# Sixteen blocks and eight products at a time, GpSimd work in pieces, and the first four destination blocks counted during the first pass

## The chip, the cores and the metric

The kernel runs on one core of a Trainium2 chip. The metric is the device time of one execution in microseconds. The kernel before has a median of 342.41 us over 4 runs (341.04 to 345.19). Lines such as L539 are lines of the kernel before, unless the text says otherwise. PE is TensorE (PEld its weight loads), DVE is VectorE, ACT is ScalarE, POOL is GpSimd, SP is SyncE.

## The reference

There are 4096 nodes with 128 features each in fp32, and 65536 edges with random ends. Each edge adds the features of its source node to the output row of its destination node:

```python
for i in range(len(edge_index_src)):
    output[edge_index_dst[i]] += node_features[edge_index_src[i]]
```

## The kernel before, in words

The kernel does no gather. It sorts the edges into cells of a 32 by 32 grid (128 source nodes by 128 destination nodes per cell), builds for each cell a count matrix by a matmul of one-hots, and multiplies the transposed features by these counts. Two passes do the sorting; both count with matmuls and move with matmuls by one-hot permutations.

**First pass, by destination block.** The 512 edge columns are handled in six quads (q = 0 to 5) of four groups of up to 22 columns. For a quad, `oh1s` compares the destination block with 32 numbers (L201, tile oh1) and sums columns on PE into `pst`; `scan` runs along them on DVE; `counts` makes running counts in PSUM (`psc`, L234 and L238), which ACT evicts (L241) and which PE sums to ranks (`psr`, L246); `spread1` multiplies the one-hots by the two payloads (L262). `move1` then does, for l = 0 to 3, three compares of ranks on DVE (L283, tile p), calls `meanwhile(l)`, and permutes with 21 or 22 matmuls into `psm` (L286). ACT copies `psm` to `sa` (a code of the source and destination within a block) and `sbk` (the source block, plus one), L290 and L291. `sbk` of all six quads is what the second pass starts from.

**Second pass, by source block.** The 32 destination blocks are taken in groups of 4, 4, 4, 4, 8 and 8 (`GROUPS`). For a group of four, `buckets4` compares `sbk` with 32 numbers (L473), `payloads` multiplies by `sa` (L415; on DVE for group 0, on POOL otherwise), `column_sums`, `sums_to_each` and `counts_ranks` give ranks (L482, L489, L496, L499, L502, `ranks` L432), `permutations` compares ranks with numbers (tiles p2a and p2c) and `permuted` moves the payloads by matmuls (L452). `quad_keys` splits the result into the low seven bits of both ends (L465, slo and dlo). The groups of eight count with 32 compares (L400), matmuls (L408), a running sum on DVE (L423) and a mask on POOL (L427).

**Block loop.** There are 32 slots: four for each four destination blocks, each with eight source blocks (32 cells). `onehots(slot)` makes two compares of 4096 columns on DVE (L201, tile oh). `blocks` multiplies them for one source block and the four destination blocks (four matmuls) into a PSUM bank `psa` (L532), and ACT casts the bank to the tile a (L534). `product` multiplies features (a high and a low part) by a into `pso` (L539), always for the slot before. A slot issues two `blocks`, four product matmuls, and so on, four times. After four slots, `evacuate` copies `pso`, and `finish` transposes it (psx, L305), copies it and sends it out by a DMA on SP.

**What sets the order.** All is scheduled by hand: each engine runs its instructions in the order in which the program text issues them, with semaphores between engines. The second pass's steps are spread over the slots by the table `STEPS` (L28): a step's first function is issued ahead of the slot's blocks, its second one behind the products, the third two slots later. Ahead of the loop, group 0 and the start of group 1 are written out (L565 to L581). Tiles with the same tag share a buffer. PSUM has two buffers each of the tags psA, pso and misc, and one each of psi and ps2. The permutation compares and the block one-hots read their numbers from PSUM (psi).

Of the kernel before, what the change touches and what calls it, by code (L numbers as in the profile page):

```python
# [8 lines left out]
P = 128  # L9
# [69 lines left out]
def _fast(ctx, tc, X, src32, dst32, out, ident, fmax, flag_i, T):  # L79
# [129 lines left out]
    def oh1s(q):  # L209

        if q % 2 == 0:
            oh1[q // 2] = sb1.tile([P, 2, NL, NB], BF16, name="oh1", tag=f"o{q // 2}")
        onehot(oh1q(q), kd[:, q], NL, NB)
        pst = ps.tile([P, 512], F32, name="pst", tag="pso")
        for j in range(NJ):
            PE.matmul(out=pst[:, j:j + 1],  # L216
                      lhsT=oh1q(q)[:, 4 * j:4 * j + 4, :].rearrange("p l b -> p (l b)"),
                      rhs=ones[:, :1], start=True, stop=True)
        sums[q] = pst
# [8 lines left out]
    def counts(q):  # L228

        cum = sb1.tile([P, NB, NL], BF16, name="cum", tag=f"c{q % 2}")  # L230
        for j0 in range(0, NJ, 4):
            n = min(4, NJ - j0)
            psc = ps.tile([P, 512], F32, name="psc", tag="psA")
            PE.matmul(out=psc[:, :n * P], lhsT=early[:],  # L234
                      rhs=oh1q(q)[:, 4 * j0:4 * (j0 + n), :].rearrange("p t b -> p (t b)"),
                      start=True, stop=j0 + n == 1)
            for j in range(max(j0, 1), j0 + n):
                PE.matmul(out=psc[:, (j - j0) * P:(j - j0 + 1) * P],  # L238
                          lhsT=sums[q][:, j - 1:j].to_broadcast([P, P]), rhs=identb[:],
                          start=False, stop=j == j0 + n - 1)  # L240
            S.activation(out=cum[:, :, 4 * j0:4 * (j0 + n)], func=RELU, bias=minus[:],  # L241
                         in_=psc[:, :n * P].rearrange("p (t b) -> p b t", b=NB))
            yield
        psr = ps.tile([P, 512], F32, name="psr", tag="pso")
        for b in range(NB):
            PE.matmul(out=psr[:, :NL], lhsT=identb[:], rhs=cum[:, b, :],  # L246
                      start=b == 0, stop=b == NB - 1)
        rank1[q] = sb2.tile([P, 4, NJ, 2], BF16, name="rank1", bufs=3)
        for k in range(2):
            S.copy(out=rank1[q][:, :, :, k], in_=psr[:, :NL].rearrange("p (j l) -> p l j", l=4))  # L250
# [25 lines left out]
    def move1(q, meanwhile):  # L276
        psm = ps.tile([P, 512], F32, name="psm", tag="misc")
        for l in range(4):
            t = p1[l // 2]
            n = len([j for j in range(NJ) if j * NCH + q * 4 + l < T])  # L280
            for j0, j1, m0, m1 in WIN:
                j1 = min(j1, n)
                onehot(t[:, l % 2, j0:j1, m0:m1], rank1[q][:, l, j0:j1], j1 - j0, m1 - m0, m0=m0)  # L283
            meanwhile(l)
            for j in range(n):
                PE.matmul(out=psm[:, l * 64:(l + 1) * 64], lhsT=t[:, l % 2, j, :],  # L286
                          rhs=v1[q][:, 4 * j + l].rearrange("p k b -> p (k b)"),
                          start=j == 0, stop=j == n - 1)
        pv = psm[:, :256].rearrange("p (l k b) -> p l k b", l=4, k=2)
        S.copy(out=sa[:, place(q), :], in_=pv[:, :, 0, :])  # L290
        S.copy(out=sbk[:, place(q), :], in_=pv[:, :, 1, :])  # L291
# [9 lines left out]
    def finish():  # L301
        for k, res in done:
            psx = ps.tile([P, 512], F32, name="psx", tag="misc")
            for i in range(4):
# [33 lines left out]
    clear(p2a)  # L338

    def during(q):  # L340

        def step(l):
            if l == 0:
                if q + 2 < NQ and q == 0:
# [8 lines left out]

    for q in range(NQ):
        move1(q, during(q))
        if q + 2 < NQ:
# [7 lines left out]

    p2c = sb1.tile([P, 2, NCH, P], BF16, name="p2c", tag="o2")
    clear(p2c)
    p2b = [p2a[:, 0], p2a[:, 1], p2c[:, 0], p2c[:, 1]]
    first = [sum(GROUPS[:g]) for g in range(len(GROUPS))]
    keys2 = {}

    def pass2(g):
# [12 lines left out]
        def tiles():  # L384
            if g == 0:
                both = sb1.tile([P, 2] + shape[1:], BF16, name="vc2", tag="o0")
                T2["v"], T2["c"] = both[:, 0], both[:, 1]
                T2["o"] = sb1.tile(shape, BF16, name="oh2", tag="o1")[:]
            else:
                at = -(g - 1) % 3  # L390
                tags = ("c0", "o1", "o0")
                T2["o"] = sb1.tile(shape, BF16, name="oh2", tag=tags[at])[:]
                T2["c"] = sb1.tile(shape, BF16, name="cum2", tag=tags[(at + 1) % 3])[:]
                T2["v"] = sb1.tile(shape, BF16, name="v2", tag="F" if g % 2 == 0 else "c1")[:]

# [8 lines left out]
        def before_all():  # L404
            psb = ps.tile([P, 512], F32, name="psb", tag="misc")
            for h in range(2):
# [3 lines left out]
            for h in range(2):  # L410
                S.copy(out=flat2(T2["c"])[:, h * NH], in_=psb[:, h * W:(h + 1) * W])

        def payloads():
            for i in range(gk):
                (V if g == 0 else G).tensor_tensor(out=T2["v"][:, :, i], in0=T2["o"][:, :, i], op=OP.mult,  # L415
                                in1=sa[:, :, None, d0 + kk * i:d0 + kk * i + kk].to_broadcast(
                                    [P, NCH, NB, kk]))

# [7 lines left out]
        def masked():  # L426
            G.tensor_tensor(out=flat2(T2["c"]), in0=flat2(T2["c"]), in1=flat2(T2["o"]), op=OP.mult)  # L427

        def ranks():
            psr = ps.tile([P, 512], F32, name="psr2", tag="misc")  # L430
            for s in range(NB):
# [13 lines left out]

        def permuted(i):
            if i % 4 == 0:
                T2["ps2"] = ps.tile([P, 512], F32, name="ps2", tag="ps2", bufs=1)
# [11 lines left out]
        def quad_keys(i):  # L460
            ks = [sb2.tile([P, 4 * NB, 2], U16, name=n) for n in ("slo2", "dlo2")]
            pau = T2["pa"][:].bitcast(U16).rearrange("p s d -> p (s d)")[
                :, :, None].to_broadcast([P, 4 * NB, 2])
            for t, arg, op in zip(ks, (7, 127), (OP.logical_shift_right, OP.bitwise_and)):
                V.tensor_single_scalar(out=t[:], in_=pau, scalar=arg, op=op)  # L465
            keys2[(d0 + i) // 4] = ks
            if i == 0:
                V.tensor_reduce(out=fmax[:, g:g + 1], in_=T2["r"][:, :, :, 0], op=OP.max,
                                axis=AX.XY)

# [8 lines left out]
        def column_sums():  # L479
            T2["p"] = ps.tile([P, 512], F32, name="pst2", tag="misc")  # L480
            for c in range(NCH):
# [10 lines left out]
        def counts_ranks():  # L492
            for c0 in range(0, NCH, 4):
                psc = ps.tile([P, 512], F32, name="psc2", tag="psA")
                cs = [c for c in range(c0, c0 + 4) if c % NH]
# [25 lines left out]
    def onehots(slot):  # L521

        oh = sb1.tile([P, 2, 4 * 8, P], BF16, name="oh", tag=f"t2{slot % 2}")
        at = slot % 4 * 32
        for k, io in ((0, piotas), (1, piota)):
            onehot(oh[:, k], keys2[slot // 4][k][:, at:at + 32], 32, io=io)
        return oh

    def blocks(k, oh, a):
        psa = ps.tile([P, 512], F32, name="psa", tag="psA")  # L530
        for i in range(4):
# [10 lines left out]
    def flag():  # L542
# [9 lines left out]
        V.tensor_reduce(out=fall[:], in_=fmax[:, :ng + 1], op=OP.add, axis=AX.X)  # L552
        psf = ps.tile([P, 512], F32, name="psf", tag="misc")
        PE.matmul(out=psf[:1, :1], lhsT=fall[:], rhs=one[:], start=True, stop=True)
        V.tensor_single_scalar(out=flag_i[:], in_=psf[:1, :1], scalar=float(P * T),
                               op=OP.not_equal)

    todo = [pass2(g) for g in range(len(GROUPS))]

# [4 lines left out]

    (vec, mat), (vec1, mat1), pair0, pair1 = todo[0]  # L565
    vec()
    mat()
    nvec, nmat = todo[1].pop(0)
    nvec1, nmat1 = todo[1].pop(0)
    vec1()  # L570
    mat1()
    nvec()
    nmat()
    pair0[0]()
    pair0[1]()
    nvec1()
    pair1[0]()
    pair1[1]()
    pair1[2]()
    oh = onehots(0)  # L580
    nmat1()  # L581
    slots = NB
    prev, pso = None, None
    late = {}
    for slot in range(slots):
# [5 lines left out]
        if slot + 1 < slots:  # L591
            oh = onehots(slot + 1)
        run(st[0] for st in steps)
        a = sb1.tile([P, 8, 4 * P], F32R, name="a", tag=f"A{slot % 2}")
        if slot % 4 == 0:
            pso = ps.tile([P, 512], F32, name="pso", tag="pso")
        for k in range(0, 8, 2):
            blocks(k, cur, a)
            blocks(k + 1, cur, a)
            if prev is not None:  # L600
                product(k, *prev)
                product(k + 1, *prev)
            if k == 0:
                finish()
        if prev is not None and prev[0] % 4 == 3:
# [100 lines left out]
```

## Time and profile before

| | |
|---|---|
| Median of 4 runs | 342.41 us (341.04 to 345.19) |
| The profiled execution | 340.93 us, its span 339.2 us |
| Busy share of the span | PE 89%, DVE 83%, ACT 59%, POOL 25% |
| Chain that ended last | PE 68%, DVE 19%, ACT 5%, issue 4%, DMA 1% |
| Mean granted clock of PE | 0.968 |
| The last `sbk` copy starts | 71.20 us |
| One-hots of slot 0 start | 87.99 us |
| Blocks of slot 0, 1, 3 start | 93.53, 101.06, 120.24 us |
| Last product group starts | 328.45 us |

The chain that ended last is followed back from the last instruction, at each step to what released it. Busy shares are means over stretches with different limits, so the timeline and the busy times of single stretches say more than the shares. A DVE or ACT row's mean is the time of one instruction; PE's matmuls overlap, so the distance between their starts says what one costs in a run.

### The profile page before, as it was taken

The page shows a single profiled execution, that of the slowest core. Times are in us where ns is not written, and L with a number is a line of the kernel's source. Part 1 is how long each engine was busy: PE and PEld are TensorE (multiplying, and loading weights), DVE is VectorE, ACT ScalarE, POOL GpSimd, SP SyncE. Part 2 cuts the span into 40 slices and gives each one's busy share as a digit, 9 for nine tenths or more (in the row PEclk, how much of TensorE's full clock was granted, in tenths as well). Part 3 has the DMA queues.
Part 4 walks back from the last instruction along what each step waited for, and adds up shares of the span by engine and source line. Part 5 has one row for each costly group of instructions (what it writes and reads, how often), then busy time and mean ns, then how long its engine had stood idle before and what let it go on. Part 6 is the DMA issues. An engine that isn't in the chain of part 4 may idle for free.

```text
span 339.2 us, 8630 instructions
## 1 busy us (share of the span) xinstructions
PE 302.3 (89%) x3784; PEld 239.2 (71%) x3784; DVE 280.4 (83%) x365; ACT 201.6 (59%) x389; POOL 84.0 (25%) x47
## 2 busy tenths in 40 slices
PE   0689899668879899999999999999999999999993
PEld 0468777456667588677788787778877778777772
DVE  4999999983899839849999898999999779868700
ACT  2776545014556856755765776575576676677761
POOL 6627000206014060000898000069900000000000
PEclk9999979858799999999999999999999999999999
DMA  8500000000000000100010000001000100100101
GB/s 240 131 2 5 2 3 2 2 2 0 5 2 0 2 2 2 31 2 3 0 33 2 0 31 5 2 1 33 2 1 4 30 2 0 33 2 0 33 2 33
DMA packets 8711, 5.81 MB, mean 17 GB/s; under 512 B 224, under 2 KB 8416, under 8 KB 8672
## 3 DMA queue, kind: packets, MB, share of 16 engines
q1 hardware_dynamic: 8528, 4.72, 4.9%
q8 instruction: 30, 0.49, 0.6%
q10 hardware_dynamic: 144, 0.52, 0.6%
q14 instruction: 9, 0.07, 0.1%
HBM read 3.15 MB, written 2.10 MB: 15 GB/s over the span
## 4 chain that ended last, share of the span: by engine, by line
PE 68%; DVE 19%; ACT 5%; issue 4%; DMA 1%; DVEq 0%; ACTq 0%
PE pso L539 33%; PE psa L532 15%; DVE oh L201 8%; PE ps L452 7%; PE psr L432 3%; PE psm L286 3%; DVE p L201 2%; DVE v L262 2%; ACT cum L502 2%; DMA raw<-in_edge_index_dst_dram 1%; DVE cum L423 1%; ACT cum L241 1%; PE psr L246 1%; PE psc L496 1%; DVE oh L400 1%
## 5 line engine op out<-in xcount | busy, mean ns | idle before, releaser
L534 ACT CAST a<-psa 128x512 fp32r<-128x512 f32 x256 | 137.7, 591 | 46.3 <-PE psa L532 45.3
L539 PE MATMUL pso<-a,xr 128*128 128x512 f32 x512 | 149.3, 414 | 0.0
L201 DVE TENSOR_TENSOR oh<-psi,slo 128x4096 bf16<-128x4096 uint16 x32 | 73.1, 2285 | 27.9 <-PE psa L532 27.9
L539 PEld LDWEIGHTS pso<-a,xr 128*128 128x128 f32 x512 | 87.0, 189 | 11.4
L532 PE MATMUL psa<-oh 128*128 128x128 bf16 x1024 | 81.2, 220 | 1.4 <-ACT a L534 0.9
L532 PEld LDWEIGHTS <-oh 128*128 128x128 bf16 x1024 | 59.3, 98 | 30.0 <-issue 28.4
L201 DVE TENSOR_TENSOR oh<-psi,dlo 128x4096 bf16<-128x4096 uint16 x32 | 72.9, 2279 | 0.0
L415 POOL TENSOR_TENSOR v<-oh,sa 128x3072 bf16<-128x3072 bf16 x7 | 37.7, 5397 | 40.3 <-DVE oh L473 31.9
L427 POOL TENSOR_TENSOR cum<-cum,oh 128x6144 bf16<-128x6144 bf16 x2 | 23.9, 11938 | 75.8 <-ACT a L534 75.8
L201 DVE TENSOR_TENSOR p<-psi,rank 128x448 bf16<-128x448 uint16 (+3 forms) x72 | 29.2, 472 | 0.0
L241 ACT ACTIVATE cum<-psc,minus 128x512 bf16<-128x512 f32 (+1 forms) x36 | 21.8, 649 | 10.6 <-PE psc L238 10.3
L286 PE MATMUL psm<-v,p 128*128 128x64 bf16 x512 | 23.0, 204 | 5.3 <-DVE p L201 4.8
L286 PEld LDWEIGHTS <-p 128*128 128x128 bf16 x512 | 20.1, 105 | 7.1 <-DVE p L201 6.9
L201 DVE TENSOR_TENSOR p2a<-psi,rank 128x768 bf16<-128x768 uint16 x32 | 15.5, 546 | 5.6 <-ACT rank L437 5.6
L238 PEld LDWEIGHTS <-sums 128*128 128x128 bf16 x126 | 11.3, 107 | 6.3 <-issue 3.2
L201 DVE TENSOR_TENSOR p2c<-psi,rank 128x768 bf16<-128x768 uint16 x32 | 15.5, 544 | 0.0
L234 PE MATMUL psc<-oh,early 128*128 128x512 bf16 (+1 forms) x36 | 14.6, 406 | 0.9 <-ACT cum L241 0.9
L190 POOL TENSOR_TENSOR xr<-xf,xr 128x512 fp32r<-128x512 f32 x8 | 11.8, 1494 | 13.3 <-ACT xr L186 13.3
L452 PEld LDWEIGHTS <-p2a 128*128 128x128 bf16 x384 | 12.8, 100 | 3.0 <-DVE p2a L201 1.8
L216 PE MATMUL pst<-ones,oh 128*128 128x1 bf16 x132 | 4.3, 164 | 11.6 <-DVE oh L201 11.5
L238 PE MATMUL psc<-identb,sums 128*128 128x128 bf16 x126 | 14.4, 240 | 0.0
L452 PEld LDWEIGHTS <-p2c 128*128 128x128 bf16 x384 | 12.9, 102 | 1.8 <-issue 1.5
(82 smaller groups left out, 273.2 us busy)
## 6 DMA issues: line engine op xcount, KB each, us to landing
xf<-in_node_features_dram SPq DMA_DIRECT2D x4, 512.0 KB, 7.4
out_dram<-rows SPq DMA_DIRECT2D x8, 256.0 KB, 2.3
raw<-in_edge_index_src_dram ACTq DMA_DIRECT2D x1, 512.0 KB, 4.8
raw<-in_edge_index_dst_dram SPq DMA_DIRECT2D x1, 512.0 KB, 5.0
```

The costliest lines, as they stand in the source:

```text
L190: G.tensor_tensor(out=xr[i // 2][:, bs, 1, :], op=OP.subtract, in0=xf[i][:, h * BX // 2:(h + 1) * BX // 2], in1=xr[i // 2][:, bs, 0, :])
L201: V.tensor_tensor(out=dst.rearrange("p i (m k) -> p i m k", k=2), in0=io.rearrange("p i (m k) -> p i m k", k=2), in1=keys2[:, :, None, :]. ...
L234: PE.matmul(out=psc[:, :n * P], lhsT=early[:], rhs=oh1q(q)[:, 4 * j0:4 * (j0 + n), :].rearrange("p t b -> p (t b)"), start=True, stop=j0 + ...
L238: PE.matmul(out=psc[:, (j - j0) * P:(j - j0 + 1) * P], lhsT=sums[q][:, j - 1:j].to_broadcast([P, P]), rhs=identb[:], start=False, stop=j = ...
L241: S.activation(out=cum[:, :, 4 * j0:4 * (j0 + n)], func=RELU, bias=minus[:], in_=psc[:, :n * P].rearrange("p (t b) -> p b t", b=NB))
L286: PE.matmul(out=psm[:, l * 64:(l + 1) * 64], lhsT=t[:, l % 2, j, :], rhs=v1[q][:, 4 * j + l].rearrange("p k b -> p (k b)"), start=j == 0, ...
L415: (V if g == 0 else G).tensor_tensor(out=T2["v"][:, :, i], in0=T2["o"][:, :, i], op=OP.mult, in1=sa[:, :, None, d0 + kk * i:d0 + kk * i + ...
L427: G.tensor_tensor(out=flat2(T2["c"]), in0=flat2(T2["c"]), in1=flat2(T2["o"]), op=OP.mult)
L452: PE.matmul(out=ps2[:, d % 4 * NB:(d % 4 + 1) * NB], lhsT=p2b[d % 4][:, c, :], rhs=T2["v"][:, c, d // kk, :, d % kk], start=c == 0, stop=c ...
L532: PE.matmul(out=psa[:, i * P:(i + 1) * P], lhsT=oh[:, 0, 4 * k + i, :], rhs=oh[:, 1, 4 * k + i, :], start=True, stop=True)
L534: S.copy(out=a[:, k, :], in_=psa[:])
L539: PE.matmul(out=pso[:], lhsT=xr[s // 16][:, s % 16, v, :], rhs=a[:, k, :], start=s == 0 and v == 0, stop=s == NB - 1 and v == 1)
```

## The change

Four things change.

1. **Sixteens and eights.** A slot issues four `blocks` (sixteen matmuls), then the products of four k (eight matmuls), twice. `psA` gets four buffers, and `pso`, `misc` and the first pass's other PSUM tags get one. `pst` of the first pass alternates between the tags ps2 and pso, `psr` uses psA. `finish` comes behind the second sixteen blocks.
2. **GpSimd in pieces.** The multiplies of groups 1 to 5 are put into a list as pieces of four columns, the masks of the groups of eight as pieces of two; `little` issues up to seven per slot, and what is left before it is needed.
3. **Group 0 quad by quad.** Group 0 no longer goes through `pass2`. While `move1` works on quads 2 to 5, `beside(q, l)` issues the bucket compares, the multiplies (on POOL, the last quad's on DVE), column sums, scans and counts of the quads that are done, and in quad 5 the ranks and the permutations of the first two destination blocks for five of the six quads. The last quad's part follows the first pass, and its result is added to the earlier part (`part0`).
4. **Head of the loop.** `onehots(0)` is made in four halves of 16, ahead of group 1's scan on DVE; group 1's `counts_ranks` come behind it. `p2c` is cleared before quad 5's move.

```diff
-        pst = ps.tile([P, 512], F32, name="pst", tag="pso")
+        pst = ps.tile([P, 512], F32, name="pst", tag=("ps2", "pso")[q % 2], bufs=1)
...
-            psc = ps.tile([P, 512], F32, name="psc", tag="psA")
+            psc = ps.tile([P, 512], F32, name="psc", tag="psA", bufs=4)
...
-        psm = ps.tile([P, 512], F32, name="psm", tag="misc")
+        psm = ps.tile([P, 512], F32, name="psm", tag="misc", bufs=1)
...
+    def buckets0(q):
+        cs = place(q)
+        V.tensor_tensor(
+            out=T0["o"][:, cs], op=OP.is_equal,
...
+        (G if q < NQ - 1 else V).tensor_tensor(
+            out=T0["v"][:, cs], in0=T0["o"][:, cs], op=OP.mult,
+            in1=sa[:, cs, None, :4].to_broadcast([P, 4, NB, 4]))
+        for c in range(cs.start, cs.stop):
+            PE.matmul(out=T0["p"][:, c:c + 1], rhs=ones[:, :1], start=True, stop=True,
+                      lhsT=T0["o"][:, c].rearrange("p s k -> p (s k)"))
...
+    def ranks0(cs):
+        n = cs.stop - cs.start
+        psr = T0["p"][:, 64 + 4 * cs.start:64 + 4 * cs.stop]
+        for s in range(NB):
+            PE.matmul(out=psr, lhsT=identb[:], rhs=T0["c"][:, cs, s, :],
+                      start=s == 0, stop=s == NB - 1)
+        for k in range(2):
+            S.copy(out=T0["r"][:, :, cs, k], in_=psr.rearrange("p (c d) -> p d c", d=4))
...
+    def beside(q, l):
+
+        if q == 2 and l == 2:
+            start0()
+            buckets0(0)
+            buckets0(1)
+        if q == 2 and l == 3:
+            scan0(0)
+            scan0(1)
+        if q == 3 and l == 0:
+            counts0(0)
+            counts0(1)
+        if q in (3, 4):
+            if l == 1:
+                buckets0(q - 1)
+            if l == 2:
+                scan0(q - 1)
+            if l == 3:
+                counts0(q - 1)
+        if q == 5:
+            if l == 0:
+                buckets0(4)
+                for cs in EARLY0:
+                    ranks0(cs)
+            if l == 1:
+                scan0(4)
+                counts0(4)
+                for cs in EARLY0:
+                    permute0((0, 1), cs)
+            if l == 2:
+                ranks0(place(4))
+            if l == 3:
+                permute0((0, 1), place(4))
+                permuted0((0, 1), done0, 0)
...
         def payloads():
             for i in range(gk):
...
+                for c in range(0, NCH, 4):
+                    small.append(((g, 1), lambda i=i, c=c: payload(i, slice(c, c + 4))))
...
         def masked():
-            G.tensor_tensor(out=flat2(T2["c"]), in0=flat2(T2["c"]), in1=flat2(T2["o"]), op=OP.mult)
+            for c in range(0, NCH, 2):
+                small.append(((g, 0), lambda c=c: G.tensor_tensor(
+                    out=flat2(T2["c"])[:, c:c + 2], in0=flat2(T2["c"])[:, c:c + 2],
+                    in1=flat2(T2["o"])[:, c:c + 2], op=OP.mult)))
...
-    (vec, mat), (vec1, mat1), pair0, pair1 = todo[0]
-    vec()
-    mat()
+    last0 = place(NQ - 1)
+    buckets0(NQ - 1)
+    scan0(NQ - 1)
+    counts0(NQ - 1)
+    for cs in done0:
+        permute0((2, 3), cs)
     nvec, nmat = todo[1].pop(0)
     nvec1, nmat1 = todo[1].pop(0)
-    vec1()
-    mat1()
     nvec()
+    ranks0(last0)
+    permuted0((2, 3), done0, 0)
+    parts = [T0["x"][:, i * P:(i + 1) * P].rearrange("p (d s) -> p s d", d=4) for i in range(2)]
+    part0 = sb1.tile([P, NB, 4], BF16, name="part0")
+    S.copy(out=part0[:], in_=parts[0])
+    for d in range(4):
+        permute0((d,), last0)
+        permuted0((d,), (last0,), P)
+    pa0 = sb2.tile([P, NB, 4], BF16, name="pa")
+    V.tensor_tensor(out=pa0[:], in0=parts[1], in1=part0[:], op=OP.add)
     nmat()
-    pair0[0]()
-    pair0[1]()
+    put_keys(0, pa0)
+    oh = onehots(0)
     nvec1()
-    pair1[0]()
-    pair1[1]()
-    pair1[2]()
-    oh = onehots(0)
     nmat1()
+    most_rank(0, T0["r"])
...
         run(st[0] for st in steps)
+        little(7)
...
-        for k in range(0, 8, 2):
-            blocks(k, cur, a)
-            blocks(k + 1, cur, a)
+        for k0 in (0, 4):
+            for k in range(k0, k0 + 4):
+                blocks(k, cur, a)
+            if k0 == 4:
+                finish()
             if prev is not None:
-                product(k, *prev)
-                product(k + 1, *prev)
-            if k == 0:
-                finish()
+                for k in range(k0, k0 + 4):
+                    product(k, *prev)
```

## The prediction

> **What bounds the kernel now.** I read the page's rows, then the stretches of the span, then the chain that ended last, then the timeline of the places that the change touches. The rows of the block loop:
>
> ```profile
> L534 ACT CAST a<-psa 128x512 fp32r<-128x512 f32 x256 | 137.7, 591 | 46.3 <-PE psa L532 45.3
> L539 PE MATMUL pso<-a,xr 128*128 128x512 f32 x512 | 149.3, 414 | 0.0
> ...
> L532 PE MATMUL psa<-oh 128*128 128x128 bf16 x1024 | 81.2, 220 | 1.4 <-ACT a L534 0.9
> ```
>
> PE's two matmul groups hardly wait (0.0 and 1.4 us), while ACT waits 45.3 us for them. The stretches (columns: stretch, us, busy us of PE, PEld, DVE, ACT, POOL, then PE's granted clock):
>
> ```profile
> 0.00:65.60 65.60, 45.93 (x914) 38.02 (x914) 60.15 (x99) 33.78 (x67) 19.82 (x34) 0.97 0.19 50
> 65.60:94.00 28.40, 22.41 (x356) 17.93 (x357) 20.66 (x34) 9.43 (x20) 8.15 (x5) 0.71 0.01 2
> ...
> 246.00:328.00 82.00, 81.95 (x823) 63.30 (x821) 63.93 (x51) 59.03 (x112) 0.10 (x1) 1.00 0.04 11
> ```
>
> So there are three regimes: a first pass bound by DVE (60.15 of 65.60), a transition bound by latency with PE at clock 0.71, and a block loop where PE is full. Inside the loop, one period of the timeline:
>
> ```profile
> 280.07 0.62 PE L532 MATMUL psa<-oh 128*128 128x128 bf16 x8
> ...
> 280.50 1.18 PE L539 MATMUL pso<-a,xr 128*128 128x512 f32 x4
> ...
> 281.52 0.62 PE L532 MATMUL psa<-oh 128*128 128x128 bf16 x8
> ...
> 328.24 4.41 PEld L539 LDWEIGHTS pso<-a,xr 128*128 128x128 f32 x20
> ```
>
> Eight blocks and four products take 281.52 - 280.07 = 1.45 us. The last 20 products, unbroken, take 4.63 us in the chain: 0.2315 each. Blocks in a run start 0.056 us apart. 8 x 0.056 + 4 x 0.2315 = 1.374, so each change from blocks to products and back costs about 0.072 us. From the chain in the transition:
>
> ```profile
> 79.10 1.27 ACT vc L502 x2
> 80.42 1.55 PE psr L432 x32
> 83.14 1.93 PE ps L452 x48
> 85.15 1.95 PE ps L452 x48
> 87.99 6.22 DVE oh L201 x3
> ```
>
> The first one-hots of the second pass start at 87.99. Group 1's counts run under them (86.92 to 93.7), slot 0's blocks start at 93.53, slot 1's at 101.06.
>
> **What the Trainium skill says.** TensorE: Matmul & The Clock Gate, "What's actually happening": the array runs at half clock unless it was busy in a free-running window of 3413 ns. The trace agrees: asked window by window, the clock is 0.50 from 65.05 to 78.70 and from 85.5 to 88.9 (multiples of 3.41), after windows with idle PE. SBUF — State Buffer, "Who interferes with whom": DVE tensor_scalar in a 2-port mode and GpSimd exclude each other for a whole instruction. The trace agrees:
>
> ```profile
> L415 POOL TENSOR_TENSOR v<-oh,sa 128x3072 bf16<-128x3072 bf16 x7 | 37.7, 5397 | 40.3 <-DVE oh L473 31.9
> ```
>
> ```profile
> L465 DVE TENSOR_SCALAR dlo<-pa x8: 281/285/5461, 87.6 to 296.1; 128x256 uint16<-128x256 uint16 x8
> ```
>
> Twice (179.8 and 240.8) dlo took 5.46 us, the length of one POOL multiply. PSUM — Partial Sum Buffer, "Specifications (TRN2)": 8 banks. Before: psi 1, psA 2, pso 2, misc 2, ps2 1; after: psi 1, psA 4, the others 1, so doubled buffers elsewhere are the price of psA's four.
>
> **The change, part by part** (sum against the profiled execution: span 339.2 us, 340.93 us in all, median of the runs 342.41).
>
> Sixteens and eights. Slots 1 to 31 lose two of their four changes each: 31 x 2 x 0.072 = -4.5 us.
>
> Four psA banks. Slots without extra work last 5.79 us; slots 7, 11, 15, 19 and 30 last 6.04, 5.91, 6.03, 5.98 and 6.00, as rank and psb copies sit ahead of the evictions with two banks only. With four I take -0.8 of the 1.0. The counts of a group stay bound by ACT (six evictions in 4.01 us, back to back), so they gain 0. DVE gets 0.9 us more lead per slot (the last block now precedes eight products, not four), so the short DVE waits of slots 14 and 16 (0.24, 0.26) give -0.2.
>
> Single pso, misc and ps2. pso is next written after 16 blocks, 0.90 us, or after a permutation's 1.5 us more; its eviction takes 0.585 plus some 0.25 of latency: 0, at worst 0.1 x 7. finish moves from the first blocks of a slot to behind its second sixteen, so seven of the eight output DMAs are issued on SP some 3 us later, beside the loop (2.3 us to landing); the last stays where it was: 0. psx in slot 5 needs misc free of the column sums: DVE's scan comes some 1.4 us into the slot, psx at 3.7: 0.
>
> GpSimd in pieces. The two dlo stalls fall from 5.46 to about 0.9 us each (5.397 / 6). Worth 0: DVE sat idle 1.21 us before 191.02 and 0.48 before 251.13 for PE, and PE's slots 11, 12, 19 and 20 show no wait. Piece overhead is not in the trace; even 0.2 x 24 us per large group hides before slot 10's ranks (the 11.9 us mask ends at 174.4, its ranks start at 183.4).
>
> Group 0 in the first pass. Rates: a compare of 512 columns 0.33 us on DVE (3072 in 1.67, 768 in 0.465), of 256 0.20; a scan 0.1; a 32-column matmul 0.031; rank copies 0.4 a pair; an eviction 0.69.
> - Quads 2 to 4, DVE: 2 x 0.33 + 2 x 0.1, then twice 0.33 + 0.1: +1.7; quad 5's first permutation compare starts at 67.35, not 65.62. PE has slack there; its column sums wait for DVE, not DVE for them. POOL's new multiplies (0.9 each) are done before the next spread of payloads on DVE, which otherwise would lose up to 0.9 (the spreads at 27.89 and 30.06, beside POOL, took 2.25 and 2.69, not 1.61).
> - Quad 5: bucket 0.33, scan 0.1. PE: column sums at 68.85, then 64 rank matmuls (2.05) and ACT: ranks at 70.75 and 71.75, for which DVE waits about 1.0. Four compares (1.3) and the remaining nine of the pass: done 74.75. Quad 4's counts, eviction, 32 rank matmuls and copies end at about 75 (warm), two compares at 75.2. In PE's order permuted0's 40 matmuls (1.25) stand ahead of the pass's last 21, which wait for them: psm ends near 77.3 against 71.0, sbk is ready at 77.8 against 71.47: +6.3. At half clock the 64- and 512-column matmuls double: up to +1.7. I take +0.8.
> - Tail from sbk: compare 0.4, sums 0.25, scan 0.2, counts 0.45, eviction 0.7, 32 rank matmuls 1.2, copies 0.4; meanwhile DVE does 1.7 of compares and group 1's buckets (1.67). Last permutations, their matmuls and the add: put_keys 5.8 us after sbk. POOL's first pieces run then, so slo waits about half a piece and dlo a whole one: +1.4, with the two themselves 0.5. One-hots start 7.7 us after sbk: near 86.3, against 87.99: 1.7 earlier.
> - But group 1's scan now stands behind one-hot 0 on DVE (4.5 us in four halves), and group 1's counts and ranks stand ahead of slot 0's blocks on PE. Before, they ran under the one-hots. So the counts start at about 91.0, ranks come 7.2 later (86.92 to 94.14 before): 98.2. The halves thus hide nothing. Then DVE: permutations 1.86, group 2's buckets 1.67, and PE's sums 0.7: slot 1 at about 102.7, against 101.06. Slot 0's blocks, 3.9 us with two banks, are under it.
> Sum of this part: +1.7 us, and both ends: -1 (all warm, POOL out of the way) to +7 (cold, with DVE waits on each round trip).
>
> Total: -4.5 - 0.8 - 0.2 + 1.7 = -3.8 us: span 335.4; from the median, 338.6.
>
> **The rivals.**
> - B, the transition costs nothing or gains up to 2 us: the clock rises early since PE has dense small matmuls from 68.9, and slo and dlo meet no piece. For: 2.05 us of unbroken rank matmuls fall into one window. Against: clock 0.50 from 65.05 to 78.70 before, even with a busy PE. Time 334 to 337.
> - C, it costs 3.5 to 7: cold clock in quad 5 (+1.7, 0.9 over mine) and again under group 1's counts (six of 0.86 against 0.67 each: +1.2; ranks +1.0), and DVE waits of 1 us more. Time 340 to 345.8. For: PE stands idle some 5 us ahead of those counts.
> - D, slower: the place is quads 2 to 5, where about twelve new round trips DVE to PE to DVE lie in two strict queues. If each makes DVE wait 0.8 us (compare to sum to scan took that order at 73.3 to 74.97), DVE loses 9 to 10 us, and the time is 346 to 349. It decides once those waits exceed 6.9 us beyond the 1.0 counted, as -5.5 + 1.7 + 6.9 = +3.1. Against: in quads 2 to 4 a triple of compares (1.19) separates each sum from its scan, and the column sums take 0.1 to 0.3.
> - That fewer changes do not help: if the 0.072 belonged to the run of products itself, 8 would cost as much per product as 4. The run of 20 at 0.2315 speaks against; it would add 4.5: 343. It is inside C's range.
>
> **How the numbers follow.** The forecast, 337 to 340: 0.42. B 0.26, C 0.25 (with the last rival), D 0.07. Over 1% faster means below 339.0, which is about what a measurement of this kernel tells from no change: B and a little more than half of the forecast, 0.50. Within 1%: the rest of it and C, 0.43. Slower 0.07. The range leaves out D, the top of C and the bottom of B: 334.5 to 343.5; the likeliest case alone is 337 to 340.
>
> **What would show it.** Plain slots (22, 23, 26 to 28) at 5.64 us, not 5.79; slots 11, 15, 19 equal to them; sbk's last copy near 78.6; one-hot 0 near 86.3; ranks of group 1 near 98.2; slot 1 near 102.7; dlo never above 1.9 us. I am wrong if a plain slot stays at 5.79, or if slot 1 starts before 100 or after 106.

## The result and the profile after

The changed kernel takes 341.99 us (median of 42 runs, 340.54 to 343.35), the kernel before 342.39 (63 runs on the same chips): ratio 0.9976, 95% interval [0.9961, 0.9991]. So the change is worth 0.8 us by the ratio (0.3 to 1.3 us by its interval), where 3.8 were forecast. The profiled execution of the changed kernel took 342.55 us, its span is 341.0; the profiled one of before happened to be the shorter (340.93). I therefore take totals from medians and ratios, and the traces only for where the time lies. Line numbers are now those of the changed kernel, for an experiment those of its own text.

The costliest rows of the page of the changed kernel, to be held against those of before:

```profile
L659 ACT CAST a<-psa 128x512 fp32r<-128x512 f32 x256 | 131.6, 603 | 47.2 <-PE psa L657 47.1
L664 PE MATMUL pso<-a,xr 128*128 128x512 f32 x512 | 133.6, 403 | 0.0
...
L657 PE MATMUL psa<-oh 128*128 128x128 bf16 x1024 | 70.5, 223 | 0.2
...
L535 POOL TENSOR_TENSOR v<-oh,sa 128x512 bf16<-128x512 bf16 x42 | 42.6, 1052 | 37.2 <-DVE oh L596 26.1
L552 POOL TENSOR_TENSOR cum<-cum,oh 128x512 bf16<-128x512 bf16 x24 | 29.5, 1250 | 68.1 <-DVE cum L547 34.7
...
L581 PE MATMUL ps<-v,p2a 128*128 128x32 bf16 x336 | 12.2, 195 | 6.2 <-DVE p2a L201 6.2
...
L547 DVE TENSOR_TENSOR cum<-cum,oh 128x512 bf16<-128x512 bf16 x22 | 16.1, 731 | 1.5 <-ACT cum L531 0.8
```

Products and blocks wait no longer than before (0.0 and 0.2 us). The loss sits in two small rows: the permutation matmuls of the second pass (L581) waited 6.2 us for their one-hots p2a on DVE, and an addition of the running sum (L547) takes 731 ns in the mean. The same two rows of the kernel before:

```profile
L452 PE MATMUL ps<-v,p2a 128*128 128x32 bf16 x336 | 12.1, 194 | 0.3 <-DVE p2a L201 0.3
...
L423 DVE TENSOR_TENSOR cum<-cum,oh 128x512 bf16<-128x512 bf16 x22 | 9.3, 425 | 0.7
```

The timeline of the changed kernel shows how the two hang together (columns: start, us, engine, line, operation, tiles, count; in brackets the idle time before and its releaser):

```profile
157.79 8.40 DVE L547 TENSOR_TENSOR cum<-cum,oh 128x512 bf16<-128x512 bf16 x11 [0.84 <-ACT cum L531]
158.81 1.33 POOL L552 TENSOR_TENSOR cum<-cum,oh 128x512 bf16<-128x512 bf16 x1 [31.77 <-DVE cum L547]
...
165.80 9.21 POOL L552 TENSOR_TENSOR cum<-cum,oh 128x512 bf16<-128x512 bf16 x8 [0.36 <-DVE cum L547]
166.10 2.28 DVE L201 TENSOR_TENSOR oh<-psi,slo 128x4096 bf16<-128x4096 uint16 x1
...
170.50 1.94 DVE L201 TENSOR_TENSOR p2a<-psi,rank 128x768 bf16<-128x768 uint16 x4
171.10 1.94 PE L581 MATMUL ps<-v,p2a 128*128 128x32 bf16 x48 [2.92 <-DVE p2a L201]
```

Before, the mask was one GpSimd instruction and followed the sum:

```profile
157.27 5.02 DVE L423 TENSOR_TENSOR cum<-cum,oh 128x512 bf16<-128x512 bf16 x11
...
162.46 11.93 POOL L427 TENSOR_TENSOR cum<-cum,oh 128x6144 bf16<-128x6144 bf16 x1 [37.42 <-ACT a L534]
...
166.60 1.94 DVE L201 TENSOR_TENSOR p2a<-psi,rank 128x768 bf16<-128x768 uint16 x4
```

In pieces, the first piece needs only the columns that the sum is done with first, so it starts while the sum is still running (158.81). From then on DVE and GpSimd take turns: an addition of 0.43 us that meets a running piece takes 1.27. The sum takes 3.4 us longer (8.40 against 5.02), and that delays the two one-hots and p2a queued behind it. PE runs out of work at 168.2, waits 2.92 us, and pays once more (columns: stretch, us, busy us of PE, PEld, DVE, ACT, POOL, then PE's granted clock, the DMA's share and GB/s):

```profile
166.00:171.00 5.00, 2.19 (x14) 1.50 (x11) 5.00 (x5) 2.30 (x5) 5.00 (x5) 1.00 0.00 0
171.00:175.00 4.00, 3.90 (x65) 3.79 (x66) 4.00 (x6) 1.43 (x3) 4.00 (x5) 0.57 0.00 0
```

The clock falls to half from 171.50 to 174.91, 3.41 us, right after that wait. The Trainium skill, TensorE: Matmul & The Clock Gate, "What's actually happening", says that an idle window of about 3.4 us leaves the array throttled and a busy one frees it. The trace agrees, although the window ahead was not wholly idle: PE was busy for 0.49 of its 3.41 us, and the clock was full again after a window of unbroken work. The same happens near 232.84 for the second group of eight (3.30 us of wait, then 3.41 us at half clock). In slots:

| slot, us | 8 | 9 | 16 | 17 | plain slots |
|---|---|---|---|---|---|
| before | 7.28 | 7.87 | 7.97 | 7.88 | 5.78 to 5.79 |
| changed | 10.48 | 8.48 | 10.86 | 8.34 | 5.61 to 5.63 |

So four slots lose 7.2 us, while the other slots together gain 7.0. The stretch from the start of slot 31 on is 0.9 us shorter, and slot 1 starts 2.5 us later. The transition's steps came close to the forecast: last sbk copy at 77.85 (78.6 was forecast), one-hots of slot 0 from 85.81 (86.3), slot 1's blocks at 103.60 (102.7). One of its waits, 5.72 us of PE for group 1's scan, will matter below:

```profile
90.34 0.24 DVE L612 TENSOR_TENSOR_SCAN sums<-ones,pst 128x12 bf16<-128x12 bf16 x2
...
90.56 0.50 PE L622 MATMUL psc<-identb,sums 128*128 128x128 bf16 x3 [5.72 <-DVE sums L612]
...
98.52 3.15 PE L657 MATMUL psa<-oh 128*128 128x128 bf16 x32
```

### The profile page after: what moved, and what is told of

Its sections match the earlier page's. It is cut to its first block, busy times and chain, and to the rows that moved or that the text cites. A ratio compares the mean times of both kernels' runs of the same rounds, so it can differ in the third digit from the quotient of the medians.

```text
span 341.0 us, 8887 instructions
## 1 busy us (share of the span) xinstructions
PE 295.5 (87%) x3880; PEld 248.2 (73%) x3880; DVE 285.8 (84%) x385; ACT 195.7 (57%) x395; POOL 99.7 (29%) x109
## 4 chain that ended last, share of the span: by engine, by line
PE 59%; DVE 28%; issue 5%; ACT 5%; DMA 2%; DVEq 0%; ACTq 0%
PE pso L664 30%; PE psa L657 15%; DVE oh L201 7%; PE ps L581 6%; DVE p L201 6%; DVE v L262 5%; DVE cum L547 5%; PE psr L560 3%; ACT cum L625 2%; DMA raw<-in_edge_index_dst_dram 2%; ACT a L659 1%; PE psx L305 1%; DVE p2a L201 1%; PE psc L622 1%; PE psc L619 1%
## 5 line engine op out<-in xcount | busy, mean ns | idle before, releaser
L664 PE MATMUL pso<-a,xr 128*128 128x512 f32 x512 | 133.6, 403 | 0.0
L201 DVE TENSOR_TENSOR oh<-psi,slo 128x4096 bf16<-128x4096 uint16 (+1 forms) x33 | 73.2, 2219 | 22.0 <-PE psa L657 21.6
L201 DVE TENSOR_TENSOR oh<-psi,dlo 128x4096 bf16<-128x4096 uint16 (+1 forms) x33 | 73.0, 2213 | 0.0
L535 POOL TENSOR_TENSOR v<-oh,sa 128x512 bf16<-128x512 bf16 x42 | 42.6, 1052 | 37.2 <-DVE oh L596 26.1
L552 POOL TENSOR_TENSOR cum<-cum,oh 128x512 bf16<-128x512 bf16 x24 | 29.5, 1250 | 68.1 <-DVE cum L547 34.7
L201 DVE TENSOR_TENSOR p2a<-psi,rank 128x768 bf16<-128x768 uint16 (+2 forms) x36 | 15.9, 501 | 4.1 <-ACT rank L565 4.1
L581 PE MATMUL ps<-v,p2a 128*128 128x32 bf16 x336 | 12.2, 195 | 6.2 <-DVE p2a L201 6.2
L625 ACT ACTIVATE cum<-psc,minus 128x512 bf16<-128x512 f32 x18 | 11.3, 693 | 10.6 <-PE psc L622 8.7
L547 DVE TENSOR_TENSOR cum<-cum,oh 128x512 bf16<-128x512 bf16 x22 | 16.1, 731 | 1.5 <-ACT cum L531 0.8
L581 PEld LDWEIGHTS <-p2a 128*128 128x128 bf16 x336 | 11.2, 102 | 8.3 <-DVE p2a L201 7.1
L201 DVE TENSOR_TENSOR p2c<-psi,rank 128x768 bf16<-128x768 uint16 (+2 forms) x36 | 15.8, 499 | 0.0
```

Of the source, the lines that this page charges most:

```text
L201: V.tensor_tensor(out=dst.rearrange("p i (m k) -> p i m k", k=2), in0=io.rearrange("p i (m k) -> p i m k", k=2), in1=keys2[:, :, None, :]. ...
L535: G.tensor_tensor(out=T2["v"][:, cs, i], in0=T2["o"][:, cs, i], op=OP.mult, in1=sa[:, cs, None, ds].to_broadcast([P, cs.stop - cs.start, N ...
L547: V.tensor_tensor(out=cums[:, :, c], in0=cums[:, :, c - 1], in1=ohs2[:, :, c - 1], op=OP.add)
L552: small.append(((g, 0), lambda c=c: G.tensor_tensor(out=flat2(T2["c"])[:, c:c + 2], in0=flat2(T2["c"])[:, c:c + 2], in1=flat2(T2["o"])[:, ...
L581: PE.matmul(out=ps2[:, d % 4 * NB:(d % 4 + 1) * NB], lhsT=p2b[d % 4][:, c, :], rhs=T2["v"][:, c, d // kk, :, d % kk], start=c == 0, stop=c ...
L625: S.activation(out=flat2(T2["c"])[:, c0:c0 + 4].rearrange("p c w -> p (c w)"), in_=psc[:], func=RELU, bias=minus[:])
```

## The experiments

Theory 1: the mask in pieces costs the gain, by its overlap with the running sum. Its rival: the time is lost elsewhere, in the transition or in a loop order that brings less than the plain slots show. Ratios are to the kernel before on the same chip, with 95% intervals.

| kernel | us | ratio | slot 1 at | slots 8 / 9 / 16 / 17 |
|---|---|---|---|---|
| changed | 341.99 | 0.9976 [0.9961, 0.9991] | 103.60 | 10.48 / 8.48 / 10.86 / 8.34 |
| e1, mask whole | 333.2 | 0.9753 [0.9726, 0.978] | 102.28 | 7.12 / 7.56 / 7.49 / 7.55 |
| e2, mask last columns first | 339.52 | 0.9954 [0.9937, 0.9972] | 102.27 | 7.12 / 7.55 / 8.38 / 7.56 |
| e3, only the loop's order and banks | 334.93 | 0.9811 [0.9785, 0.9838] | 100.92 | 7.12 / 7.55 / 8.26 / 7.55 |
| e4, only the pieces | 350.93 | 1.0246 [1.0209, 1.0284] | 100.98 | 10.06 / 9.34 / 11.34 / 9.35 |
| e5, mask whole, old loop order | 340.35 | 0.9947 [0.9924, 0.997] | 101.68 | 7.28 / 7.71 / 8.22 / 7.73 |
| e8, mask last first, multiplies whole | 339.26 | 0.9913 [0.9887, 0.9939] | 104.40 | 7.12 / 7.56 / 8.39 / 7.56 |
| e9, no pieces | 336.65 | 0.9848 [0.9803, 0.9893] | 104.88 | 7.12 / 7.52 / 8.39 / 7.55 |
| e7, e1 with the scan first | 330.95 | 0.969 [0.9647, 0.9734] | 99.55 | as e1 |
| e10, e1 with the last quad's move first | 331.79 | 0.9708 [0.967, 0.9746] | 102.79 | as e1 |
| e11, e1 with both | 329.53 | 0.9631 [0.9586, 0.9677] | 97.98 | as e1 |

**e1, the mask whole again** (the multiplies stay in pieces):

```diff
-            for c in range(0, NCH, 2):
-                small.append(((g, 0), lambda c=c: G.tensor_tensor(
-                    out=flat2(T2["c"])[:, c:c + 2], in0=flat2(T2["c"])[:, c:c + 2],
-                    in1=flat2(T2["o"])[:, c:c + 2], op=OP.mult)))
+            G.tensor_tensor(out=flat2(T2["c"]), in0=flat2(T2["c"]), in1=flat2(T2["o"]), op=OP.mult)
```

> The changed kernel with the mask of the groups of eight in one GpSimd instruction again; the multiplies stay in pieces. Theory 1 (the mask's pieces start while DVE's running sum still runs, the two take turns[...], the sum goes from 5.0 to 8.4 us and PE then waits 2.9 and 3.3 us for p2a and gets a half-clock window): the running sum is back at 5.0 us, slots 8 and 16 last 7.1 to 7.4, about 335 us. Theory 2 (sixteens and eights make PE ask for p2a too early for DVE, the pieces have no part in it): slots 8 and 16 still wait 2 to 3 us, 341 us.

Its timeline, at the place shown above:

```profile
156.47 5.02 DVE L547 TENSOR_TENSOR cum<-cum,oh 128x512 bf16<-128x512 bf16 x11 [0.84 <-ACT cum L531]
...
161.66 11.93 POOL L551 TENSOR_TENSOR cum<-cum,oh 128x6144 bf16<-128x6144 bf16 x1 [35.91 <-DVE cum L547]
...
165.80 1.94 DVE L201 TENSOR_TENSOR p2a<-psi,rank 128x768 bf16<-128x768 uint16 x4
```

The mask again starts after the sum, p2a comes at 165.80, PE's matmuls behind it at 166.71 without a wait, and the time falls by 2.2% of before, 7.6 us, by the ratios. So the first theory holds: slots 8 and 16 are back at 7.12 and 7.49 us.

**e2, the same twelve pieces, last columns first**, so that no piece can start before the sum ends:

```diff
-            for c in range(0, NCH, 2):
+            for c in range(NCH - 2, -2, -2):
```

> The changed kernel with the same twelve mask pieces, issued from the last columns to the first, so that the first piece needs the end of the running sum. Theory 1: as with the whole mask, about 335 us, running sum 5.0 us, although the pieces are as many. Theory 3 (it is the number of pieces, with their overhead and GpSimd's later end, that costs): no better than the changed kernel, 342 us.

The sum is back at 5.0 us and slots 8 and 9 at 7.12 and 7.55, so the overlap is gone. But by the ratios less than 1 of the 8 us came back, not the 335 us of the first theory: slots 11, 14, 16 and 19 take 6.2 us more than in e1. A second loss, which no theory of mine held, shows in the timeline:

```profile
175.07 12.12 POOL L535 TENSOR_TENSOR v<-oh,sa 128x512 bf16<-128x512 bf16 x12
...
178.27 9.07 DVE L412 TENSOR_SCALAR slo<-pa 128x256 uint16<-128x256 uint16 x1
```

slo did not get in at the end of the piece that was running: that piece and eight more ended before it did, and it was done when GpSimd had run dry. Slots 11 and 19 then take 8.16 and 8.00 us (5.62 in e1), as their one-hots are late. The changed kernel has the same at 183.01, behind four further pieces, but its slots 11 and 19 take 5.61 and 5.62 us, so there it costs nothing:

```profile
L412 DVE TENSOR_SCALAR slo<-pa x8: 271/288/4233, 84.2 to 298.2; 128x256 uint16<-128x256 uint16 x8
```

**e3 and e4, one part alone on the kernel before.** e3 takes the order of the loop and the PSUM buffers, e4 the pieces.

> The kernel before with sixteens and eights and the four psA banks alone. Theory 1: the loop's slots gain about 8 us together as in the changed kernel (plain slots 5.61), no wait in slots 8 and 16: 334 to 335 us. Theory 2: slots 8 and 16 wait for p2a by 2 to 3 us each: 340 us. The sum of the prediction for this part was -5.5, so 337.

> The kernel before with GpSimd in pieces alone (masks and the multiplies of groups 1 to 5). Theory 1: running sum 8.4 us, slots 8 and 16 wait for p2a by 2.4 and 3.4 us, and half a window of clock: 347 to 349 us. Theory 2: 342 to 343 us. The prediction had 0 for this part.

The loop's order and banks alone bring 1.9% (6.4 us); the pieces alone cost 2.5%, which is 2 to 4 us above the range of the first theory. Each trace has a window at half clock near slot 1 that before doesn't have (from 100.26 and 101.91), and slot 1 takes 8.43 and 8.88 us, not 7.31. In e4 the sum's additions take 1.27 us every second time, PE waits 2.34 and 3.63 us in slots 8 and 16, and slo takes 2.97 us twice.

**e5, the old loop order in e1**: `blocks`, `blocks`, `product`, `product`, with `finish` behind the first pair.

> The changed kernel with the mask whole and the loop order of before (eight blocks, then four products, finish behind the first blocks); group 0 quad by quad, the four psA banks and the multiplies in pieces stay. Theory 1 (group 0 in the first pass brings nothing by slot 3, the loop's order nearly all): 340 to 342 us, ratio 0.995 to 1.002. Theory 2 (half of the gain is due to the four banks and the earlier evictions, not to the order): slots of 5.7 us or less with the old order, ratio 0.985 to 0.990. Theory 3 (group 0's new place gains or costs 1.5 us or more): ratio below 0.99 with plain slots still at 5.78, or above 1.004.

The ratio is at the edge of the first theory's range. Plain slots are back at 5.76 to 5.79 us: the order is worth 0.155 us a slot. Slots 7, 11, 15 and 19 take 5.76 to 5.78, not 6.04, 5.91, 6.03 and 5.98: that part does not come with the order; the four banks are left as its reason, which no run tests alone. The tail after the start of slot 31 is 14.9 us, not 15.7, with the old order as well: up to the issue of the last output DMA it takes 11.56 us in both, and the DMA lands after 2.30 us instead of 3.10. Slot 5 takes 14.41 us against 13.20 in e1, and psx waits 0.82 us in it, for DVE's scan of column sums that lie in the single misc buffer: with the old order, the single buffer costs what it doesn't with the new.

**e8 and e9, the multiplies whole**: e8 with the mask pieces of e2 issued in a row, e9 with no piece at all.

```diff
-                for c in range(0, NCH, 4):
-                    small.append(((g, 1), lambda i=i, c=c: payload(i, slice(c, c + 4))))
+                payload(i, slice(0, NCH))
```

> The changed kernel with the twelve mask pieces of each group of eight issued back to back, last columns first, and the multiplies of the payloads whole again (so mask pieces and the running sum do not overlap, and fewer pieces are queued on GpSimd). Theory 1 (the mask pieces cost only by overlapping the running sum; the DVE key instruction waits because many pieces stand in a row behind it): the running sum stays at 5.0 us, slots 8 and 9 at 7.1 and 7.6, and if the keys wait it is for one long multiply of 5.4 us in slots 11 and 16 to 19 as in the kernel with only the loop changed: 333 to 335 us, ratio 0.975 to 0.981. Theory 2 (any mask in pieces costs on GpSimd's side, whatever its order, and a key instruction that meets a row of pieces waits for all of it): keys wait 9 us again, 338 to 340 us, ratio 0.990 to 0.996.

> The changed kernel with no pieces on GpSimd at all: masks and multiplies each one instruction, as before the change. Theory 1 (the pieces are worth nothing but for the keys' stall): about 0.7 us above the kernel with only the mask whole (ratio 0.9753 there), since dlo waits 5.46 us twice again and slot 16 gets a wait of 0.7: ratio 0.976 to 0.980. Theory 2 (the multiplies in pieces themselves cost or save more): ratio below 0.973 if pieces of multiplies cost, above 0.983 if they save much.

e9 is 0.95% (3.2 us) above e1, not the 0.7 us I expected. In the traces it loses 2.6 us by slot 1, and 0.3 and 0.9 in slots 14 and 16. The first is the transition: group 1's multiply stands on GpSimd just when group 0's keys are asked for.

```profile
82.97 5.37 POOL L535 TENSOR_TENSOR v<-oh,sa 128x3072 bf16<-128x3072 bf16 x1 [11.37 <-ACT rank L393]
...
84.44 4.05 DVE L412 TENSOR_SCALAR slo<-pa 128x256 uint16<-128x256 uint16 x1
```

The one-hots of slot 0 start at 88.61. In e1 the same slo takes 0.74 us and they start at 86.08. So multiplies in pieces are worth 3 us, two thirds of them in the transition. e8 hit the number of its second theory, although the overlap is gone (slots 8 and 9 at 7.12 and 7.56 us). It has the loss of e9 in the transition (slo 4.06 us, slot 1 at 104.40), and slo waits 7.67 us twice, past the end of one whole multiply to the end of the next, which adds 1.15 us in slot 11 and 0.99 in slot 19.

**e7, e10 and e11, two orders of the transition.** All have the mask whole.

```diff
-    oh = onehots(0)
     nvec1()
+    oh = onehots(0)
```

```diff
-                permuted0((0, 1), done0, 0)
...
     last0 = place(NQ - 1)
+    permuted0((0, 1), done0, 0)
```

> The changed kernel with the mask whole and group 1's scan ahead of the one-hots of slot 0 on DVE; the permutation matmuls of group 0 stay where the change put them. The kernel with only the mask whole had a ratio of 0.9753 to before, that with both moves 0.9631. Theory 1 (most of the 4 us comes from group 1's counts, which with the late scan stand between slot 0's blocks and slot 1): ratio 0.963 to 0.967, slot 1 starts near 99. Theory 2 (most comes from the permutation matmuls, which hold up the last quad's move and the last sbk copy): ratio 0.971 to 0.975, slot 1 near 101.5.

> The changed kernel with the mask whole and the permutation matmuls of the first two destination blocks of group 0 behind the last quad's move; group 1's scan stays behind the one-hots of slot 0. Theory 1 (scan): the last sbk copy starts about 1 us earlier, but slot 1 gains 1 us or less: ratio 0.971 to 0.975. Theory 2 (permutation matmuls): ratio 0.963 to 0.968, slot 1 near 99.

> The changed kernel with the mask whole, and two moves of the transition: group 1's scan ahead of the one-hots of slot 0 on DVE, as in the kernel before, and the permutation matmuls of the first two destination blocks of group 0 behind the last quad's move instead of ahead of its last part. Theory 1 (the transition's loss of 2 us at slot 1 is the order of these two steps): the last sbk copy starts 1 us earlier, slot 1 starts at 99 to 101 instead of 102.3, and the time is 330 to 332 us, ratio 0.967 to 0.972. Theory 2 (the scan delays slot 0's one-hots by as much as it brings group 1's counts forward, and the matmuls of the move only change place): 333 to 334 us, ratio 0.974 to 0.979.

e11's timeline, for the place shown of the changed kernel:

```profile
84.48 0.24 DVE L608 TENSOR_TENSOR_SCAN sums<-ones,pst 128x12 bf16<-128x12 bf16 x2
84.64 1.20 DVE L201 TENSOR_TENSOR oh<-psi,slo 128x2048 bf16<-128x2048 uint16 x1
84.70 0.50 PE L618 MATMUL psc<-identb,sums 128*128 128x128 bf16 x3 [1.31 <-DVE sums L608]
...
91.51 2.97 PE L653 MATMUL psa<-oh 128*128 128x128 bf16 x32
```

With the scan first (e7, e11), group 1's counts run under the one-hots again and PE waits 1.31 us for the scan, not 5.72; slot 1 moves from 102.28 (e1) to 99.55 (e7). The other move brings the last sbk copy forward by 1.1 us (78.12 to 76.98 in e10, 76.45 in e11), and slot 1 from 99.55 to 97.98 on top of e7. e10's own trace shows slot 1 at 102.79, later than e1's: PE's clock was at half until 98.94 in it, in e1's until 94.47. The intervals of e7 and e10 overlap each other's and, narrowly, e1's, so what each move is worth alone is not settled by the times; that of e11 lies clear of e1's. e7's ratio lies between its two theories, and e11 came out below the range of its better one. e11 is the best version: 3.7% below before.

**e12 and e13, when a key instruction gets in.** A key instruction is the tensor_scalar on DVE that makes slo or dlo. Both runs put, behind the end of e11, chains of multiplies like those of the kernel on GpSimd, and beside each a compare on DVE of chosen length, then a tensor_scalar of slo's form. Core of e12:

```diff
+    for n in range(1, 31):
+        b = sa[:, 0:4, None, 0:4].to_broadcast([P, 4, NB, 4])
...
+        onehot(lf[:, 0, :n, :], lk[:].rearrange("p c s k -> p (c s k)").bitcast(U16)[
...
+        V.tensor_single_scalar(
...
+        for c in (4, 8, 12):
+            G.tensor_tensor(out=lv[:, c:c + 4], in0=lo[:, c:c + 4], in1=b, op=OP.mult)
```

> The kernel with both moves, and behind its end 30 chains of five back-to-back GpSimd multiplies of 128x512 (1.05 us each), beside each of which DVE makes a compare of 128 to 3840 columns and then the key instruction (tensor_scalar, 128x256 uint16), so that the key instruction asks at 30 different phases of a piece. Its time is not compared; the output is that of the reference. Theory 1 (a key instruction that is asked while a piece runs gets in at that piece's end only for some phases; in the kernels so far it got in when 0.28 to 0.61 us or 0.97 to 0.99 us of the piece were left, and otherwise, with 0.05, 0.78 to 0.87 and 2.2 us left, it waited until GpSimd had nothing queued): the 30 instances split into two kinds, about 0.5 to 1.2 us and as long as the rest of the chain (2 to 4 us), sorted by the phase at which they ask. Theory 2 (chance, or something else that differs between those kernels): the two kinds are mixed over the phases.

The tile's row (duration in ns: least, median, most):

```profile
L763 DVE TENSOR_SCALAR le<-lp x30: 268/684/1190, 315.1 to 464.6; 128x256 uint16<-128x256 uint16 x30
```

My theory of the phase is wrong. All 30 got in at the end of the running piece (of the next one where only 0.03 us were left), none waited longer than 1.19 us. There, a key instruction came, and got in, every five pieces. e13 makes the rows longer:

> The kernel with both moves, and behind its end 16 chains of back-to-back GpSimd pieces of 128x512 with no wait between them. In each, m = 2, 4, ... 16 pieces run, then DVE, busy with compares until then, asks for the key instruction (tensor_scalar, 128x256 uint16, its input written by ACT), and six or so multiplies still follow. In the first eight chains the m pieces are multiplies of a broadcast row, in the other eight they are of the mask's form (three plain bf16 operands). Its time is not compared; the output is that of the reference. Theory 1 (a long row of pieces without a wait, some twelve or more, shuts the key instruction out until GpSimd has nothing queued, as in the kernels with the mask in pieces): short waits of 0.3 to 1.2 us for small m, 4 to 6 us from some m of 8 to 12 on, in both forms. Theory 2 (the mask's form does it, not the number): short waits in the first eight chains, long ones in the other eight. Theory 3 (neither): short waits in all 16, and the cause of the long waits stays open.

```profile
428.69 0.28 DVE L788 TENSOR_SCALAR ls<-lt 128x256 uint16<-128x256 uint16 x1
428.77 5.13 POOL L782 TENSOR_TENSOR ly<-lo,sa 128x512 bf16<-128x512 bf16 x5
...
436.32 15.12 POOL L780 TENSOR_TENSOR lv<-lo,sa 128x512 bf16<-128x512 bf16 x15
...
451.23 6.39 DVE L788 TENSOR_SCALAR ls<-lt 128x256 uint16<-128x256 uint16 x1
451.39 5.08 POOL L782 TENSOR_TENSOR ly<-lo,sa 128x512 bf16<-128x512 bf16 x5
```

At 428.69, in the 14th piece of a row, it got in at once (0.28 us); at 451.23, in the 16th, it stood through five more pieces and a sixth from 456.41 on, 6.39 us. Rows of 2 to 14 multiplies and of 2 to 13 mask pieces let it in after 0.28 to 1.20 us, those of 16, and of 15 and 17, after 6.39, 5.78 and 5.42. So it is the row's length and not the form of the pieces: the first theory of e13, though its edge lies later than I expected. It fits the kernels: at the 13th to 18th instruction of a row that had lasted 16.7 to 18.5 us, slo was shut out (the changed kernel, e2, e4, e8); at the 2nd to 7th of a row that had lasted up to 17.3 us, slo and dlo were let in (before, e1, e3, e9). Time alone doesn't sort these cases: after 16.65 us, slo was let in at the 6th instruction in e1 and shut out at the 16th in e2. Nor does the number alone: the 14th let it in after 13.99 us in e13, and the 13th, in e8, shut it out after 16.66. What in the hardware does it stays open.

## Why the prediction was wrong

**The step that failed is "GpSimd in pieces ... Worth 0".** It asked only whether the mask, grown by the pieces' overhead, would still end before its readers, slot 10's ranks; it did. It didn't ask what the first piece would now overlap. The piece starts as soon as the sum is done with its columns, inside the running sum, and the two engines then hold each other up. The Trainium skill, SBUF — State Buffer, "Who interferes with whom", says that a DVE instruction with two SBUF inputs contends with a GpSimd instruction that reads SBUF, since its second input comes through a read interface that they share. The trace agrees: 0.43 us becomes 1.27. I quoted that section for tensor_scalar alone. The mask's part of the step, put at 0, measures +8.4 us in slots 8, 9, 16 and 17, changed kernel against e1 (7.6 us by the ratios).

**The same step was also wrong the other way.** I saw no worth in shorter key stalls, as slots 11, 12, 19 and 20 showed no wait before. But with group 0 moved, a whole multiply lies in the transition (e9: 2.6 us by slot 1). "dlo never above 1.9 us" held for dlo, but slo took 4.23: I took for granted that a waiting instruction gets in at the next piece's end.

**Sixteens and eights, banks, lead: mechanism right, size too small.** The sum was -5.5. From before to e1, the start of slot 1 to that of slot 31 shrinks from 222.43 to 214.10 us, by 8.3. The order has its 0.155 us a slot (-4.8 over 31 slots; 0.144 predicted, and 0.152 by the rounded figures that the prediction shows, 1.45 - 1.374 = 0.076 for each change). Slots 7, 11, 15 and 19 have the 0.8 to 0.9 that I put down to the banks. What I left out or made too small: slot 2 (11.87 to 11.26), slot 5 (13.96 to 13.20), slot 14 (8.65 to 8.24), and the slots with psx (7.87 to 7.53), each more than the order's 0.155. Slot 16 falls too, from 7.97 to 7.49, but with the multiplies in pieces: it takes 8.26 us in e3 and 8.39 in e9. The tail also falls, from 15.71 to 14.82 us, but only 0.12 of that lies ahead of the issue of the last output DMA. The rest is its landing (3.10 us before, 2.83 in e3, 2.29 in e1), for which no run shows the cause.

**Group 0: +1.7 predicted, +1.2 to +2.5 at slot 1** (e1 and the changed kernel, which there differ by how long the clock was at half: until 94.47 and 99.82). By slot 3, e1 (120.69) stands where e3 with the old transition stands (120.62), but e3 has its window at half clock on the way, so the tie is partly luck. The reason I gave, group 1's scan behind the one-hots, is borne out by e7's trace: taking it away brings 2.7 us at slot 1.

**Rivals.** B did not come: slot 1 is later than before, not earlier. C came in part: in the changed kernel the clock stood at half from 79.34 to 99.82, and group 1's ranks took 2.72 us on PE, not 1.53. But slot 1 lost 2.5 us, and C had 3.5 to 7. That the time itself, 341.99, lies in C's range is luck: the loss is in slots 8, 9, 16 and 17, where C had none. D did not happen: the last sbk copy started at 77.85 where 78.6 was forecast, so in all the new round trips in quads 2 to 5 cost no more than counted. That fewer changes do not help is refuted by e3 and e5. With the mask's cost left out, the parts and the tail sum to about -8, which e1's ratio shows. None of my rivals had a loss in the pieces.

## What to carry to other kernels

Cutting an instruction into pieces also lets its first piece start earlier: before calling it free, look at what that piece will now run beside, and whether the two share ports or a queue leads from the slowed one to the bottleneck. A gain of a few us spread over many slots can vanish in four slots, so compare slot by slot before doubting the gain. Cut the GpSimd work that a short DVE instruction meets, but not into one long unbroken row.

## What the runs showed of the hardware

- A tensor_scalar on DVE (128x256, uint16) that meets a row of GpSimd instructions usually gets in at the end of the running one (done after 0.27 to 1.20 us in e12 and in 13 of the 16 chains of e13). It was held until GpSimd ran dry, up to 9.07 us, wherever it met the 13th or a later instruction of a row that had lasted 15.9 us or more, counted from GpSimd's last pause or from the last such tensor_scalar that got in. The Trainium skill, SBUF — State Buffer, "Who interferes with whom", says that the one that comes second is blocked for the whole instruction of the other; here it was blocked for the rest of the running one and up to eight more (e2).
- A PE wait of 2.92 us was followed by a further window of 3.41 us at half clock, so that a delay of 3.4 us on DVE became some 4.3 us in slots 8 and 9 of the changed kernel against e1. Not every wait of 2 us or more has one: e4's of 2.34 us had, e2's of 2.39 and 2.23 us had not.
- Pieces of 128x512 (bf16) take 1.05 us on GpSimd for the multiply, and 1.16 for the mask where they run undisturbed; twelve masks make 13.5 us in e2, where the whole one takes 11.93.
